# Layer 1's mixer: u tiles first, z tiles in pairs by Strassen's form, then the pool products

## The chip, the cores and the metric

The kernel runs on one core of one Trainium2 chip. The metric is the device time of one execution in microseconds (us).

## The reference

Two layers over 1024 latent tokens of width 1024, in float32. Layer 0 is a bidirectional mLSTM, which the change leaves as it is. Layer 1 is a pooling mixer, cut here to its core (the tokens are a grid of 16 rows by 64 columns; windows are 2, 4, 8 and 16, each for a group of 512 of the 2048 inner channels):

```python
u, z = split(h @ w_in, 2)                       # 1024 -> 2 x 2048
for g, w in enumerate((2, 4, 8, 16)):
    d[g] = box_mean(box_mean(u[g], w, columns), w, rows) - u[g]
y[g] = (d[g] @ w_pool[g]) * pool_scale          # 512 -> 512 in each group
out = (y * silu(z)) @ w_out
```

Around it stand a norm before (its result is h), a norm behind, and a gated residual.

## The kernel before

All data are channels on 128 partitions by tokens. Each product is made of float32 values split in a high and a low part, so one product of a 128 x 128 weight block is three matmuls (`mm3`, its matmuls have line L136) of 512 tokens. `load_w` (L138) loads a weight tile through SP's queue into `wr`, makes the high part on ScalarE (L142, `wh`) and the low part on VectorE (L144, `wl`); there are two buffers of each.

Layer 1 takes h (the tiles `h2`, 16 buffers of the tag S4: two token halves, four pairs of channel blocks, high and low) and makes 16 u tiles and 16 z tiles of 128 channels, each 2 halves x 8 blocks x 3 matmuls, then 16 pool tiles of 2 x 4 x 3. A u tile is copied by ScalarE twice from PSUM: into `U` (L1084, padded for the window) and `ur` (L1085). `box` (L1092) makes the box sums with shifted additions on VectorE: along the columns (L1097), along the rows (L1101), the scaling by the window's count (L1105, or L1109 to L1111 for window 16) and the difference from u (L1106, L1112); then the high part `a` (ScalarE, L1114) and the low part `b` (VectorE, L1115). A z tile is Silu from PSUM into `sz` (L1090). A pool tile multiplies, scales by `sz` on VectorE (L1166) and, but for the last group, stores y by POOL's queue (L1168).

The groups come one after the other: group 0's u and z tiles by halves (the second half's norm, `norm0`, is spread over the first half's matmuls by `tick`; `drain` ends it), the groups 1 to 3 whole, in the order

```python
ORDER_B = ("u0", "u1", "b0", "u2", "b1", "u3", "z0", "b2", "z1", "b3", "p0", "z2", "p1", "z3", "p2", "p3")
```

PE's order is written out by hand (`manual_schedule`) to the end of group 0's z tiles (`ctx1.close()`); elsewhere, and on the other engines and queues throughout, a planner orders the instructions. Buffers are taken by tag: `S4` has 32 of 4 KB a partition, `T5` 5, `pt` 6, `wr`, `wh` and `wl` 2 each; PSUM has `pa` 3, `pb` 2 and `pc` 3.

Layer 0 already computes its z and o tiles in pairs by a Strassen form with 7 half-size products for 8 (`strassen`, L573): weight sums on POOL, splits of each product's weights (L593), sums of products on VectorE (L601). The sums of the token blocks that it multiplies (T1, T2, T3, T4, split high and low) are made by `block_sums` (L519), stored, and loaded again by `load_sums` (L566).

Of the kernel before, what the change touches and what calls it, by code (L numbers as in the profile page):

```python
# [51 lines left out]
def hybrid_block(ctx: ExitStack, tc: tile.TileContext, xT, ctxT, vecs, w_ada0, w_ada, w_blk, w_krow, blk_mask, w_gate, w_in, b_gate, w_out,  # L52
# [490 lines left out]
    with ctx0:  # L543
# [29 lines left out]
        def strassen(src, done):  # L573


            r1, r2 = tl("wr", [P, 8, P]), tl("T5", [P, 8, P])
            nc.sync.dma_start(r1, src[0])
            nc.sync.dma_start(r2, src[1])
            a11, a12, a21, a22 = r1[:, :4], r1[:, 4:], r2[:, :4], r2[:, 4:]
            s12, s34 = tl("T5", [P, 2, 4, P]), tl("T5", [P, 2, 4, P])  # L580
            s1, s2, s3, s4 = s12[:, 0], s12[:, 1], s34[:, 0], s34[:, 1]
            G.tensor_tensor(s1, a21, a22, op=ALU.add)
            G.tensor_tensor(s2, s1, a11, op=ALU.subtract)
            G.tensor_tensor(s3, a11, a21, op=ALU.subtract)
            G.tensor_tensor(s4, a12, s2, op=ALU.subtract)
            wt = []

            def product(tag, a, b):
                i = len(wt) % 2
                wt.append((tl("wh", [P, 2, 4, P], F32R), tl("wl", [P, 2, 4, P], F32R)) if i == 0 else wt[-1])  # L590
                hi, lo = (t[:, i] for t in wt[-1])
                S.activation(hi, a, AF.Copy)  # L592
                V.tensor_tensor(lo, a, f(hi), op=ALU.subtract)  # L593
                p = pt_(tag)
                for k in range(4):
                    mm3(p, hi[:, k], lo[:, k], *b[k], k == 0, k == 3)
                return p

            def plus(p, t, d=None):
                d = tl("pt", [P, 512]) if d is None else d  # L600
                V.tensor_tensor(d, p, t, op=ALU.add)  # L601
                return d

            p = product("pa", a11, b11)
            p1 = tl("pt", [P, 512])
            S.activation(p1, p, AF.Copy)
            done(0, 0, plus(product("pc", a12, b21), p1))
            u2 = plus(product("pa", s2, tpart(2)), p1, p1)
            u3 = plus(product("pc", s3, tpart(3)), u2)
            p = product("pa", s1, tpart(1))  # L610
            done(1, 1, plus(p, u3))
            plus(p, u2, u2)
            done(1, 0, plus(product("pc", a22, tpart(4)), u3, u3))
            done(0, 1, plus(product("pa", s4, b22), u2, u2))

# [453 lines left out]
    def u_start(g):  # L1069
# [8 lines left out]
        return U, tl("S4", [P, T]), R_, C_, r0, hw  # L1078

    def u_half(ut, w, hf):  # L1080
        U, ur, R_, C_, r0, hw = ut
        p = pt_("pa")
        h2mm(p, w, hf)
        S.activation(U[:, r0 + 8 * hf:r0 + 8 * hf + 8, hw:], p.rearrange("p (r c) -> p r c", c=64), AF.Copy)  # L1084
        S.activation(ur[:, hf * 512:(hf + 1) * 512], p, AF.Copy)  # L1085

    def z_half(sz, w, hf):
        p = pt_("pc")
        h2mm(p, w, hf)
        S.activation(sz[:, hf * 512:(hf + 1) * 512], p, AF.Silu)  # L1090

    def box(ut, g, imv):  # L1092
        U, ur, R_, C_, r0, hw = ut
        win = WINDOWS[g]
# [24 lines left out]
    for g in range(4):  # L1119
        imap = tl("T5", [P, T])  # L1120
        nc.sync.dma_start(imap, inv_cnt[g:g + 1].to_broadcast([P, T]))
        imv = imap.rearrange("p (r c) -> p r c", c=64)
        ut, szs, d = [None] * 4, [None] * 4, []
        if g == 0:
            for hf in range(2):
                for j in range(4):
                    if hf == 0:
                        ut[j] = u_start(g)
                    u_half(ut[j], load_w(bw_in[4 * g + j]), hf)
                    if hf:  # L1130
                        d.append(box(ut[j], g, imv))
                for j in range(4):
                    if hf == 0:
                        szs[j] = tl("S4", [P, T])
                    z_half(szs[j], load_w(bw_in[KE + 4 * g + j]), hf)
                if hf == 0:
                    drain()
            ctx1.close()

        def u_tile(j):  # L1140
            w = load_w(bw_in[4 * g + j])
            ut[j] = u_start(g)
            for hf in range(2):
                u_half(ut[j], w, hf)

        def z_tile(j):
            w = load_w(bw_in[KE + 4 * g + j])
            szs[j] = tl("S4", [P, T])
            for hf in range(2):
                z_half(szs[j], w, hf)  # L1150

        def pool_tile(j):
# [141 lines left out]
```

## Time and profile before

| | us |
|---|---|
| median of 3 runs | 2021.52 |
| lowest and highest | 2017.68, 2022.14 |
| the profiled execution | 2018.94 |
| its span, first to last instruction | 2017.2 |
| PE (TensorE) busy in it | 1970.4 |

The profile is of one execution. PE is TensorE's matmuls, PEld its weight loads, DVE VectorE, ACT ScalarE, POOL GpSimd, SP SyncE, which only issues transfers; PEq, SPq and POOLq are the queues. The clock is the share of full speed that TensorE was granted.

### The profile page before, as it was taken

The page shows a single profiled execution, that of the slowest core. Times are in us where ns is not written, and L with a number is a line of the kernel's source. Part 1 is how long each engine was busy: PE and PEld are TensorE (multiplying, and loading weights), DVE is VectorE, ACT ScalarE, POOL GpSimd, SP SyncE. Part 2 cuts the span into 40 slices and gives each one's busy share as a digit, 9 for nine tenths or more (in the row PEclk, how much of TensorE's full clock was granted, in tenths as well). Part 3 has the DMA queues.
Part 4 walks back from the last instruction along what each step waited for, and adds up shares of the span by engine and source line. Part 5 has one row for each costly group of instructions (what it writes and reads, how often), then busy time and mean ns, then how long its engine had stood idle before and what let it go on. Part 6 is the DMA issues. An engine that isn't in the chain of part 4 may idle for free.

```text
span 2017.2 us, 26878 instructions
## 1 busy us (share of the span) xinstructions
PE 1970.4 (98%) x10050; PEld 1662.4 (82%) x10050; DVE 1287.7 (64%) x2140; ACT 807.1 (40%) x1353; POOL 419.6 (21%) x620
## 2 busy tenths in 40 slices
PE   6999999999999999999999999999999999999997
PEld 4788888788888788888888878888888888888897
DVE  4777777777767677676676662746745382943454
ACT  5477777333333433323332322534422231223443
POOL 2144434354443111111111110200000000000154
PEclk9999999999999999999999999999999999999999
DMA  9377777844444847446372414525331213142573
GB/s 365 126 256 268 266 266 269 305 157 147 131 141 142 317 136 238 154 139 232 110 261 100 152 59 156 214 92 174 95 115 56 89 42 105 43 160 100 188 241 125
DMA packets 118292, 339.49 MB, mean 168 GB/s; under 512 B 13036, under 2 KB 21740, under 8 KB 118160
## 3 DMA queue, kind: packets, MB, share of 16 engines
q1 hardware_dynamic: 90144, 242.14, 35.2%
q0 software_dynamic: 28016, 95.62, 12.8%
q8 instruction: 79, 1.29, 0.3%
q14 instruction: 53, 0.43, 0.1%
HBM read 234.77 MB, written 102.94 MB: 167 GB/s over the span
## 4 chain that ended last, share of the span: by engine, by line
PE 90%; DMA 3%; DVE 3%; ACT 2%; issue 1%; POOL 1%; SPq 0%; POOLq 0%; DVEq 0%; ACTq 0%
PE pa L136 46%; PE pc L136 35%; PE pb L136 7%; PE pb L803 2%; DVE S L923 1%; PE pc L834 1%; DMA S<-in_w_ada_dram 1%; DVE wl L144 1%; DMA S<-in_ctxT_dram 1%; DMA S<-a_d 0%; POOL S L1011 0%; DMA wr<-in_w_ada_dram 0%; DMA T<-in_bw_out_dram 0%; DMA cst<-in_w_blk_dram 0%; ACT wh L142 0%
## 5 line engine op out<-in xcount | busy, mean ns | idle before, releaser
L136 PE MATMUL pa<-S,wh 128*128 128x512 f32 (+1 forms) x2448 | 705.2, 372 | 0.0
L136 PEld LDWEIGHTS pa<-S,wh 128*128 128x128 f32 x2448 | 434.7, 189 | 67.9
L136 PE MATMUL pc<-S,wh 128*128 128x512 f32 (+1 forms) x1664 | 465.6, 366 | 3.0 <-ACT wh L142 2.2
L136 PE MATMUL pa<-S,wl 128*128 128x512 f32 (+1 forms) x1224 | 450.4, 368 | 0.0
L136 PEld LDWEIGHTS pc<-S,wh 128*128 128x128 f32 x1664 | 302.2, 190 | 54.4 <-ACT wh L142 2.4
L136 PE MATMUL pc<-S,wl 128*128 128x512 f32 (+1 forms) x832 | 303.1, 366 | 0.8 <-DVE wl L144 0.7
L144 DVE TENSOR_TENSOR wl<-wr,wh 128x1024 fp32r<-128x1024 f32 (+1 forms) x124 | 144.1, 1162 | 249.3 <-ACT wh L142 248.0
L142 ACT ACTIVATE wh<-wr 128x1024 fp32r<-128x1024 f32 (+1 forms) x124 | 124.7, 1005 | 356.8 <-PE pa L136 136.3
L136 PEld LDWEIGHTS pa<-S,wl 128*128 128x128 f32 x1224 | 230.9, 189 | 40.1 <-DVE wl L144 0.5
L136 PE MATMUL pa<-S,S 128*128 128x512 f32 (+1 forms) x1152 | 249.7, 363 | 4.3 <-DVE T L762 4.3
L136 PE MATMUL pc<-S,pt 128*128 128x512 f32 x960 | 227.6, 391 | 1.5 <-DVE S L743 1.0
L136 PEld LDWEIGHTS pa<-S,S 128*128 128x128 f32 x1152 | 192.0, 190 | 33.4 <-DVE T L762 4.5
L136 PEld LDWEIGHTS pc<-S,pt 128*128 128x128 f32 x960 | 178.0, 188 | 38.4 <-DVE S L743 1.7
L136 PEld LDWEIGHTS pc<-S,wl 128*128 128x128 f32 x832 | 157.9, 190 | 26.8 <-DVE wl L144 2.1
L805 ACT ACTIVATE pt<-pb 128x512 fp32r<-128x512 f32 (+1 forms) x96 | 47.8, 524 | 214.9 <-PE pb L803 212.6
L762 DVE SCALAR_TENSOR_TENSOR T<-pa,T 128x256 f32<-128x256 f32 (+3 forms) x184 | 78.3, 453 | 33.4 <-PE pa L136 27.2
L957 POOL TENSOR_TENSOR r4b<-r,mhalf 128x4 f32<-128x4 f32 (+1 forms) x7 | 9.2, 1320 | 389.4 <-DVE r L955 389.4
L425 ACT ACTIVATE T<-pb 128x288 f32<-128x288 f32 x160 | 63.0, 416 | 42.3 <-PE pb L136 31.9
L136 PE MATMUL pb<-S,wh 128*128 128x512 f32 x256 | 78.8, 389 | 0.0
L592 ACT ACTIVATE wh<-T 128x512 fp32r<-128x512 f32 x70 | 41.2, 626 | 93.5 <-PE pc L136 76.4
L816 DVE BATCH_NORM_STATS2 st<-pc 128x6 f32<-128x512 f32 x32 | 22.3, 698 | 83.7 <-PE pc L136 83.7
L144 DVE TENSOR_TENSOR wl<-T,wh 128x1024 fp32r<-128x1024 f32 x32 | 45.5, 1423 | 37.6 <-ACT wh L142 37.6
(341 smaller groups left out, 2606.9 us busy)
## 6 DMA issues: line engine op xcount, KB each, us to landing
wr<-in_bw_in_dram SPq DMA_DIRECT2D x40, 512.0 KB, 3.6
wr<-in_w_in_dram SPq DMA_DIRECT2D x34, 512.0 KB, 4.2
wr<-in_w_ada_dram SPq DMA_DIRECT2D x32, 512.0 KB, 4.0
wr<-in_w_out_dram SPq DMA_DIRECT2D x32, 512.0 KB, 3.6
T<-in_bw_out_dram SPq DMA_DIRECT2D x32, 512.0 KB, 4.5
S<-y_d SPq DMA_DIRECT2D x28, 512.0 KB, 7.4
vh_d<-T POOLq DMA_DIRECT2D x32, 320.0 KB, 4.7
vl_d<-T POOLq DMA_DIRECT2D x32, 320.0 KB, 4.3
```

What stands on the lines that cost most here:

```text
L136: PE.matmul(out, lhsT, rhs, start=start, stop=stop)
L142: S.activation(h, r, AF.Copy)
L144: V.tensor_tensor(l, r, f(h), op=ALU.subtract)
L425: S.activation(vst[:, :, s - s0], p, AF.Copy)
L592: S.activation(hi, a, AF.Copy)
L762: V.scalar_tensor_tensor(W[:, lo + sh:hi + sh], p[:, lo - o:hi - o], 1.0, W[:, lo + sh:hi + sh], op0=ALU.mult, op1=ALU.mult, accum_out=dp[ ...
L803: PE.transpose(p[:, j], st["M"][:, s * P:(s + 1) * P], ident)
L805: S.activation(th[:, :n], p[:, :n], AF.Copy)
L816: V.bn_stats(b6, pv)
L834: PE.transpose(p[:, c], hn[:, c * P:(c + 1) * P], ident)
L923: V.tensor_tensor(b, yraw[kp, hf], f(a), op=ALU.subtract)
L957: G.tensor_tensor(r2[:, :nb], r[:, :nb], mhalf[:, :nb], op=ALU.pow)
```

## The change

Layer 1 is ordered anew in three parts. First come all 16 u tiles, groups 3 and 2 by halves (weights loaded twice), then groups 1 and 0; each half is copied into `pt` and stored to `u_d`. The boxes of groups 3 and 2 are made beside them from u loaded back, and their high and low parts are stored (`dh_d`, `dl_d`). Beside them too, `block_sums1` makes the sums of h's blocks from `o_d`, which `next_input` now stores, and stores them in `t1_d`. Second come the z tiles, in 8 pairs by `strassen`, now an outer function; the parts 2 and 3 of T1 are loaded among the last u tiles, 1 and 4 in the first pair; Silu of z is stored in `sz_d`. Third come the pool products of groups 3, 2, 1, 0, with d and `sz` loaded back; the boxes of group 1 are made beside group 3's products and those of group 0 beside group 2's. PE's order is by hand through all of it. y of group 0 stays in SBUF, the others go through `y2_d`.

The diff, without the new DRAM tiles, the unchanged body of `strassen` that is moved, and the removed forms of the old loop:

```diff
+    def strassen(src, done, blocks, tpart, tag2):
...
+        b11, b21, b22 = blocks
+        r1, r2 = tl("wr", [P, 8, P]), tl(tag2, [P, 8, P])
...
         for n in range(0, KE, 2):
-            prod = strassen if n else plain
+            def prod(src, done):
+                if n:
+                    strassen(src, done, (b11, b21, b22), tpart, "T5")
+                else:
+                    plain(src, done)
...
+                if j:
+                    nc.gpsimd.dma_start(o_d[k - 1:k + 1, :, 512 * hf:512 * hf + 512].rearrange("j p t -> p j t"), x1[kp])
...
+    def u_half(n, w, hf):
+        p = pt_("pc" if n % 2 else "pa")
+        h2mm(p, w, hf)
+        t = tl("pt", [P, 512])
+        S.activation(t, p, AF.Copy)
+        nc.gpsimd.dma_start(u_d[n, :, hf * 512:hf * 512 + 512], t)
+
+    imvs = {}
+
+    def box(n):
+        g = n // 4
+        if g not in imvs:
+            imap = tl("T5", [P, T])
+            nc.sync.dma_start(imap, inv_cnt[g:g + 1].to_broadcast([P, T]))
+            imvs[g] = imap.rearrange("p (r c) -> p r c", c=64)
+        imv = imvs[g]
         win = WINDOWS[g]
         hw = win // 2
         R_, C_ = (16 if win == 16 else 16 + hw), 64 + hw
         r0 = R_ - 16
-        U = tl("T5", [P, R_, C_])
+        U, ur = tl("T5", [P, R_, C_]), tl("S4", [P, T])
+        nc.sync.dma_start(ur, u_d[n])
...
+        S.activation(U[:, r0:, hw:], ur.rearrange("p (r c) -> p r c", c=64), AF.Copy)
...
-        a, b = tl("S4", [P, T], F32R), tl("S4", [P, T], F32R)
+        a = tl("S4", [P, T], F32R)
         S.activation(a, ur, AF.Copy)
-        V.tensor_tensor(b, ur, f(a), op=ALU.subtract)
-        return a, b
+        nc.gpsimd.dma_start(dh_d[n], f(a))
+        V.tensor_tensor(ur.bitcast(F32R), ur, f(a), op=ALU.subtract)
+        nc.gpsimd.dma_start(dl_d[n], ur)
+
+    def block_sums1():
+        dsh1 = const([P, 4], "dsh1")
+        V.tensor_tensor(dsh1, sh1[:, 4:8], sh1[:, 0:4], op=ALU.subtract)
+        for k in range(4):
+            t0, t1 = tl("S4", [P, T]), tl("S4", [P, T])
+            for t, kk in ((t0, k), (t1, k + 4)):
+                nc.sync.dma_start(t, o_d[kk])
+            b11, b12, b21, b22 = t0[:, :512], t0[:, 512:], t1[:, :512], t1[:, 512:]
+            V.scalar_tensor_tensor(b22, b22, dsh1[:, k:k + 1], b12, op0=ALU.add, op1=ALU.subtract)
+            V.tensor_tensor(b12, b12, b11, op=ALU.subtract)
+            V.scalar_tensor_tensor(b11, b22, sh1[:, k:k + 1], b11, op0=ALU.add, op1=ALU.add)
+            V.scalar_tensor_tensor(b21, b21, sh1[:, k + 4:k + 5], b11, op0=ALU.add, op1=ALU.subtract)
+            yield
+            for j, x in ((2, b11), (3, b22), (1, b12), (4, b21)):
+                t = tl("S4", [P, 2, 512], F32R)
+                S.activation(t[:, 0], x, AF.Copy)
+                V.tensor_tensor(t[:, 1], x, f(t[:, 0]), op=ALU.subtract)
+                nc.gpsimd.dma_start(t1_d[j - 1, k], f(t))
+                if j in (3, 4):
+                    yield
+
+
+    order = [4 * g + j for g in (3, 2, 1, 0) for j in range(4)]
+    boxes = iter(order)
+    for hf in range(2):
+        for i, n in enumerate(order[:8]):
+            u_half(n, load_w(bw_in[n]), hf)
+            if hf:
+                next(sums1, None)
+                if i % 2:
+                    box(next(boxes))
+        if hf == 0:
+            drain()
+            sums1 = block_sums1()
+    T1_ = {}
+
+    def load_sums1(j):
+        for k in range(4):
+            T1_[j, k] = tl("S4", [P, 2, 512], F32R)
+            nc.sync.dma_start(f(T1_[j, k]), t1_d[j - 1, k])
+
+    for i, n in enumerate(order[8:]):
+        w = load_w(bw_in[n])
+        for hf in range(2):
+            u_half(n, w, hf)
+        next(sums1, None)
+        if i % 2 == 0:
+            box(next(boxes))
+        if i in (5, 6):
+            load_sums1(i - 3)
+
+
+    h2b = [[(h2[hf, k // 2][0][:, k % 2], h2[hf, k // 2][1][:, k % 2]) for k in range(ko, ko + 4)]
+           for ko, hf in ((0, 0), (4, 0), (4, 1))]
+
+    def sz_done(n, i, hf, t):
+        S.activation(t, t, AF.Silu)
+        nc.gpsimd.dma_start(sz_d[n + i, :, hf * 512:hf * 512 + 512], t)
+
+    def tpart1(j):
+        if (j, 0) not in T1_:
+            load_sums1(j)
+        return [(T1_[j, k][:, 0], T1_[j, k][:, 1]) for k in range(4)]
+
+    for n in range(0, KE, 2):
+        strassen([bw_in[KE + n + i] for i in range(2)], lambda i, hf, t: sz_done(n, i, hf, t), h2b, tpart1, "T5")
 
...
+    for g in (3, 2, 1, 0):
+        d = []
+        w = load_w(bw_pool[4 * g], 4)
+        for k in range(4):
+            pair = [tl("S4", [P, T], F32R) for _ in range(2)]
+            for t, src_ in zip(pair, (dh_d, dl_d)):
+                nc.sync.dma_start(f(t), src_[4 * g + k])
+            d.append(pair)
+        for j in range(4):
             n = 4 * g + j
+            if j:
+                w = load_w(bw_pool[n], 4)
             for hf in range(2):
                 s_ = slice(hf * 512, hf * 512 + 512)
+                sz = tl("pt", [P, 512])
+                nc.sync.dma_start(sz, sz_d[n, :, s_])
+                p = pt_("pc" if j % 2 else "pa")
                 for k in range(4):
                     mm3(p, w[0][:, k], w[1][:, k], d[k][0][:, s_], d[k][1][:, s_], k == 0, k == 3)
+                if g:
+                    o = sz
                 else:
                     if n % 2 == 0:
                         yraw[n // 2, hf] = tl("S4", [P, 2, 512])
                     o = yraw[n // 2, hf][:, n % 2]
+                V.scalar_tensor_tensor(o, p, vc("pool_scale", n), sz, op0=ALU.mult, op1=ALU.mult)
+                if g:
+                    nc.gpsimd.dma_start(y2_d[n - 4, :, s_], o)
+            if g > 1:
+                for _ in range(2 if j % 2 == 0 else 0):
+                    box(next(boxes))
+    ctx1.close()
...
-        for kp in range(6):
+        for kp in range(2, 8):
             yraw[kp, hf] = tl("S4", [P, 2, 512])
-            nc.sync.dma_start(yraw[kp, hf], y2_d[2 * kp:2 * kp + 2, :, s_].rearrange("j p t -> p j t"))
+            nc.sync.dma_start(yraw[kp, hf], y2_d[2 * kp - 4:2 * kp - 2, :, s_].rearrange("j p t -> p j t"))
```

## Rows read from the trace of the kernel before

**Rows 1.** The page's first part, and the span and clock of the core.
```profile
PE 1970.4 (98%) x10050; PEld 1662.4 (82%) x10050; DVE 1287.7 (64%) x2140; ACT 807.1 (40%) x1353; POOL 419.6 (21%) x620
...
core 0: 2017.2 us, clock 0.992
```

**Rows 2.** Windows: us, busy (count) of PE, PEld, DVE, ACT, POOL; clock, DMA share, GB/s.
```profile
510.19:529.24 19.05, 19.05 (x86) 15.78 (x85) 12.57 (x18) 6.90 (x13) 8.22 (x7) 1.00 0.46 152
1421.74:1813.26 391.52, 391.52 (x1729) 324.27 (x1728) 225.31 (x217) 105.78 (x152) 16.63 (x44) 1.00 0.26 86
655.00:660.00 5.00, 5.00 (x24) 4.14 (x23) 1.54 (x4) 0.63 (x1) 0.34 (x1) 1.00 1.05 404
680.00:685.00 5.00, 5.00 (x17) 3.92 (x16) 1.49 (x10) 5.00 (x11) 0.82 (x4) 0.67 1.02 417
1953.00:1958.00 5.00, 4.48 (x19) 4.19 (x20) 2.79 (x3) 1.69 (x3) 0.00 (x0) 0.51 0.92 362
1816.00:1818.00 2.00, 1.63 (x7) 1.05 (x6) 2.00 (x3) 2.00 (x4) 0.00 (x0) 1.00 0.71 227
```

**Rows 3.** The chain of waits, from 1595 us: start, us, what.
```profile
1595.82 43.52 PE pa L136 x192
```

**Rows 4.** VectorE's groups by line and shape: count, busy us, mean ns, idle before.
```profile
L593 DVE TENSOR_TENSOR wl<-T,wh 128x512 fp32r<-128x512 f32 x69 | 47.3, 708 | 0.0
L601 DVE TENSOR_TENSOR pt<-pc,pt 128x512 f32<-128x512 f32 x41 | 28.3, 691 | 43.4 <-PE pc L136 43.2
...
L1115 DVE TENSOR_TENSOR S<-S,S 128x1024 fp32r<-128x1024 f32 x16 | 19.5, 1221 | 10.6 <-ACT S L1114 10.6
```

**Rows 5.** POOL's issues of y's stores: ns min/median/max, first and last start.
```profile
L1168 POOL DMA_DIRECT2D y_d<-pt x24: 540/540/597, 1469.5 to 1705.7; - x24
```

**Rows 6.** Transfers issued between 1373 and 1814: count, KB, median us to landing.
```profile
wr<-in_bw_in_dram SPq DMA_DIRECT2D x37, 512.0 KB, 3.6
y_d<-pt POOLq DMA_DIRECT2D x24, 256.0 KB, 2.5
```

**Rows 7.** VectorE's timeline in boxes of windows 16, 8 and 4.
```profile
1717.55 5.28 DVE L1097 TENSOR_TENSOR T<-T 128x1136 f32<-128x1136 f32 x4
1722.86 4.00 DVE L1101 TENSOR_TENSOR T<-T 128x960 f32<-128x960 f32 x4
...
1728.43 0.69 DVE L1109 TENSOR_TENSOR T<-T,T 128x512 f32<-128x512 f32 x1
...
1732.72 1.22 DVE L1112 TENSOR_TENSOR S<-T,S 128x1024 f32<-128x1024 f32 x1
...
1608.75 3.82 DVE L1097 TENSOR_TENSOR T<-T 128x1072 f32<-128x1072 f32 x3
1612.60 4.08 DVE L1101 TENSOR_TENSOR T<-T 128x1216 f32<-128x1216 f32 x3
...
1499.95 2.49 DVE L1097 TENSOR_TENSOR T<-T 128x1040 f32<-128x1040 f32 x2
1502.47 2.55 DVE L1101 TENSOR_TENSOR T<-T 128x1088 f32<-128x1088 f32 x2
```

**Rows 8.** ScalarE's timeline in group 3, idle before and its releaser in brackets.
```profile
1731.92 0.60 ACT L1084 ACTIVATE T<-pa 128x512 f32<-128x512 f32 x1 [3.69 <-PE pa L136]
1734.04 1.06 ACT L1114 ACTIVATE S<-S 128x1024 fp32r<-128x1024 f32 x1 [1.52 <-DVE S L1112]
1735.00 0.58 ACT L1085 ACTIVATE S<-pa 128x512 f32<-128x512 f32 x1
...
1756.48 1.07 ACT L1114 ACTIVATE S<-S 128x1024 fp32r<-128x1024 f32 x1 [6.94 <-DVE S L1112]
1757.45 1.07 ACT L1085 ACTIVATE S<-pa 128x512 f32<-128x512 f32 x2
```

**Rows 9.** SP's timeline in layer 0, the loads of T1's parts.
```profile
345.28 19.16 SPq L566 DMA_DIRECT2D S<-t_d  x14
```

**Rows 10.** The page's second part: GB/s in 40 equal slices of the span.
```profile
GB/s 365 126 256 268 266 266 269 305 157 147 131 141 142 317 136 238 154 139 232 110 261 100 152 59 156 214 92 174 95 115 56 89 42 105 43 160 100 188 241 125
```

More of the change, by code (lines that the diff above doesn't have):

```diff
@@ L132, in hybrid_block @@
     x1_d = dr.tile([P, KD, T], F32, name="x1_d")
+    o_d = dr.tile([KD, P, T], F32, name="o_d")
+    t1_d = dr.tile([4, 4, P, 2, 512], F32, name="t1_d")
+    u_d = dr.tile([KE, P, T], F32, name="u_d")
+    dh_d = dr.tile([KE, P, T], F32, name="dh_d")
+    dl_d = dr.tile([KE, P, T], F32, name="dl_d")
+    sz_d = dr.tile([KE, P, T], F32, name="sz_d")
     y2_d = dr.tile([12, P, T], F32, name="y2_d")
@@ L440, in token_part, with product, plus @@
                 mm(gacc[ci][:32, :w], gx, ch, False, n == KE - 1)
+    def strassen(src, done, blocks, tpart, tag2):
+        b11, b21, b22 = blocks
+        r1, r2 = tl("wr", [P, 8, P]), tl(tag2, [P, 8, P])
+        nc.sync.dma_start(r1, src[0])
+        nc.sync.dma_start(r2, src[1])
+        a11, a12, a21, a22 = r1[:, :4], r1[:, 4:], r2[:, :4], r2[:, 4:]
+        s12, s34 = tl("T5", [P, 2, 4, P]), tl("T5", [P, 2, 4, P])
+        s1, s2, s3, s4 = s12[:, 0], s12[:, 1], s34[:, 0], s34[:, 1]
+        G.tensor_tensor(s1, a21, a22, op=ALU.add)
+        G.tensor_tensor(s2, s1, a11, op=ALU.subtract)
+        G.tensor_tensor(s3, a11, a21, op=ALU.subtract)
+        G.tensor_tensor(s4, a12, s2, op=ALU.subtract)
+        wt = []
+        def product(tag, a, b):
+            i = len(wt) % 2
+            wt.append((tl("wh", [P, 2, 4, P], F32R), tl("wl", [P, 2, 4, P], F32R)) if i == 0 else wt[-1])
+            hi, lo = (t[:, i] for t in wt[-1])
+            S.activation(hi, a, AF.Copy)
+            V.tensor_tensor(lo, a, f(hi), op=ALU.subtract)
+            p = pt_(tag)
+            for k in range(4):
+                mm3(p, hi[:, k], lo[:, k], *b[k], k == 0, k == 3)
+            return p
+        def plus(p, t, d=None):
+            d = tl("pt", [P, 512]) if d is None else d
+            V.tensor_tensor(d, p, t, op=ALU.add)
+            return d
+        p = product("pa", a11, b11)
+        p1 = tl("pt", [P, 512])
+        S.activation(p1, p, AF.Copy)
+        done(0, 0, plus(product("pc", a12, b21), p1))
+        u2 = plus(product("pa", s2, tpart(2)), p1, p1)
+        u3 = plus(product("pc", s3, tpart(3)), u2)
+        p = product("pa", s1, tpart(1))
+        done(1, 1, plus(p, u3))
+        plus(p, u2, u2)
+        done(1, 0, plus(product("pc", a22, tpart(4)), u3, u3))
+        done(0, 1, plus(product("pa", s4, b22), u2, u2))
     emt = const([P, 8, 36], "emt")
@@ L571, in hybrid_block @@
         b11, b21, b22 = ([h[k + ko, hf] for k in range(4)] for ko, hf in ((0, 0), (4, 0), (4, 1)))
[L573 to L614, printed above, removed]
         def z_done(n, sz, i, hf, t):
@@ L1077, in u_start @@
         G.memset(U[:, r0:, 0:hw], 0.0)
[L1078 to L1094, printed above, removed]
+        S.activation(U[:, r0:, hw:], ur.rearrange("p (r c) -> p r c", c=64), AF.Copy)
         st = 1
@@ L1112, in box @@
             V.tensor_tensor(urv, M_, urv, op=ALU.subtract)
-        a, b = tl("S4", [P, T], F32R), tl("S4", [P, T], F32R)
+        a = tl("S4", [P, T], F32R)
         S.activation(a, ur, AF.Copy)
-        V.tensor_tensor(b, ur, f(a), op=ALU.subtract)
-        return a, b
-    yraw = {}
[L1119 to L1152, printed above, removed]
@@ new lines, in tpart1 @@
+    def tpart1(j):
[4 more added lines that the diff above has]
+        strassen([bw_in[KE + n + i] for i in range(2)], lambda i, hf, t: sz_done(n, i, hf, t), h2b, tpart1, "T5")
+    yraw = {}
+    for g in (3, 2, 1, 0):
+        d = []
+        w = load_w(bw_pool[4 * g], 4)
+        for k in range(4):
+            pair = [tl("S4", [P, T], F32R) for _ in range(2)]
[3 more added lines that the diff above has]
+        for j in range(4):
```

16 lines of the change are left out of this document (removed).

## The prediction

> **What bounds the kernel now.** First the page's busy times [rows 1]: TensorE (PE) is busy 1970.4 of 2017.2 us, 98%, at a mean granted clock of 0.992; VectorE has 64%, ScalarE 40%. So the span is what TensorE is given, plus its pauses. Then the windows [rows 2]: from the start of layer 1's second token half at 1421.74 to 1813.26, where the last pool product ends, PE is busy for all 391.52 us, with 225 us of VectorE and only 86 GB/s of DMA. The stage to be changed has no pause to win, only matmuls to drop. Then the chain of waits [rows 3]: 192 matmuls of 512 columns take 43.52 us, 226.7 ns each, in the new stage too if nothing waits. The other rows tell what the new work around them costs.
>
> All sums stand against the profiled execution: 2017.2 us of span and 1.7 around it, 2018.9. The three runs go from 2017.68 to 2022.14, median 2021.52, so it is 0.1% under the median. About 0.2%, 4 us, is what can be told from no change here.
>
> **Part 1, the matmuls.** A pair of z tiles takes 2 x 48 = 96 matmuls now; Strassen's form takes 7 products of 12, 84. Eight pairs save 96 x 0.2267 = 21.8 us. Layer 0 shows what such a pair takes: 84 matmuls in 19.05 us without a pause, with VectorE busy 12.57 of it and POOL 8.22 [rows 2]. In the new z stage VectorE has 7 splits of 0.71 and 7 sums of 0.69 for each pair [rows 4], 9.8 us of 19.05; pairs 2 to 8 should run at 19.05. The pause behind the last pool product, 0.37 of the 2.00 us from 1816 [rows 2], may go with y of one group staying in SBUF: 0.4. **-22.2 us.**
>
> **Part 2, box sums behind the u tiles and the first z pair.** Eight wide groups' boxes now run beside 130.6 us of u tiles (t = 0 at the second half pass; 8 x 5.44 + 8 x 10.88). A box no longer takes u from PSUM: ScalarE copies it out (0.59), POOL issues a store (0.54) that lands 2.5 us later [rows 5, 6], SP loads it back (3.6, as a weight load of the same size), ScalarE copies it into U (1.06). Box 12 starts at 5.44 + 0.59 + 0.54 + 2.5 + 3.6 + 1.06 = 13.7.
>
> To its high part `a`, a box of window 16 costs VectorE 5.28 + 4.00 + 3 x 0.69 + 1.22 = 12.6, one of window 8 3.82 + 4.08 + 2 x 1.22 = 10.3 [rows 7]: 91.6 us for eight. Other VectorE work in the stage: 14 weight splits and 8 low parts of a box, both of 1024 columns and 1.22, 27, and block sums, 32 operations of 512 columns and 0.69 [rows 4], 22: 49.
>
> Between boxes there is a gap that before did not have. The trace shows buffers of one tag being given out in program order: with half of S4's 32 buffers free, ScalarE's second copy of u (L1085) starts at 1735.00 though its twin from the same PSUM tile (L1084) ran at 1731.92; in between stands the previous box's `a` at 1734.04, whose buffer is asked for earlier in the program. At 1757.45 two such copies again stand right behind an `a` [rows 8]. By that order a box's reload is placed behind the `a` of the box before: 3.6 + 1.06 + 0.3, 5 us, seven times, 35. So the last wide box ends between 13.7 + 91.6 + 35 = 140 (all other work fits in the gaps) and 13.7 + 91.6 + 35 + 49 = 189 (none does). I take the middle, 164, 34 us after the u tiles' end.
>
> What is late next is the first z pair. T1 parts 3, 1 and 4 stand behind box 11's `a` in the same tag, and SP has the second pair's weights (whose T5 buffer is the window map that box 11 reads last) ahead of them. They are 12 loads of 512 KB: 14 such took 19.16 us in layer 0 [rows 9], 1.37 each; at the 266 GB/s of the mixed slices in the page's fourth to seventh slice [rows 10] 1.97. I take 1.7: 20.4, and 2 to land. Product 6 needs the last of them, then come 3.4 us of matmuls: the pair ends 34 + 20.4 + 2 + 3.4 = 60 after the u tiles instead of 19. **+41 us**; with 140 and 1.37 it is 9.4 + 16.4 + 5.4 - 19 = 12, with 189 and 1.97 it is 58.4 + 23.6 + 5.4 - 19 = 68.
>
> **Part 3, the pool products, 87.0 us of PE.** Their inputs now come from DRAM: d 24 x 0.524 MB for three groups (the first group's can come in the z stage), eight reloads of u 4.2, dh and dl stores 8.4, sz 8.4, y2 6.3, pool weights 4.2, yraw 3.1: 47 MB. At some 400 GB/s, the best 5 us windows (404 and 417 [rows 2]), this takes 118 us, 31 more than PE; at 417 and without yraw 18. Before, this whole stage moved 86 GB/s.
> The order of buffers makes a chain of it as well. Box 4's reload can start when the last z pair's second product has freed h2's buffers, 13.6 us before the stage, so the box starts at -8.6. Four boxes of window 4 (2.49 + 2.55 + 2 x 1.22 = 7.5 each [rows 7]), three low parts and eight evictions of 0.7 to 0.75 put the last `a` at -8.6 + 30 + 3.7 + 5.5 = 31. The next group's d stands behind it in the tag: 8 loads at 1.37 less a first product's 2.7 and 2 to land, 10. Group 2 starts at 41 and not 21.8: 19. Boxes 0 to 3 stand behind these loads: 11 + 5 to the first, 4 x 4.9 (four operations of 1.22) + 3.7 + 4 to the last `a`, 10 for d: 53 after 31, against 41 + 21.8: 21. So 40 with no gap between boxes, 70 with gaps of 5. I take **+39**, near the low end, since it is also nearest to the bytes' 31; bounds 18 and 70.
> The Trainium skill ("HBM Reference", Specifications (TRN2)) gives about 358 GB/s as a core's effective share of HBM; by it, as an estimate, the 47 MB take 131 us and the stall is 44. This trace's windows at 404 and 417 GB/s lie above that figure, as the same page of the Trainium skill says of a core that streams alone, so the rows decide.
>
> **Part 4, the clock after a pause.** Where PE starts again after a pause the granted clock is low: 17 matmuls between 680 and 685 at 0.67, where 226.7 ns would make 22, and 0.51 between 1953 and 1958 [rows 2]. That is 1 to 3 us for each long pause; with some three of them **+4** (1 to 6).
>
> **At nothing.** POOL's extra work: 72 issues of 0.54 beside the u tiles (u 32, o 8, T1 16, dh and dl 16), 39 of 130 us, and 8.2 of 19.05 us in a pair; behind a late store only the box that reloads it waits, already counted. ScalarE's extra copies, 1.06 for a box and 0.6 for half a u tile, lie beside 391 us of which it is busy for 106 [rows 2]; without that cover each would add itself to a box. The moved norm0 of half 1 keeps its place beside the first half pass, with 4 more POOL issues.
>
> **Sum.** 2018.9 - 22.2 + 41 + 39 + 4 = 2080.7, **2080**.
>
> **Rivals.**
> (a) *Boxes end in time, the pool stage alone stalls.* If other work fits in the gaps and SP's queue lets reloads go ahead of the `a` (the order is shown on ScalarE's own queue, not across to SP), box 11 ends by some 140 and the first pair loses 12 or less. 2018.9 - 22.2 + 6 + 29 + 2 = 2034, about 2015 to 2050. For it: SP's loads do not wait for ScalarE. Against: the seven reloads still need their u copies on ScalarE behind the `a`.
> (b) *Faster: reloads and d run ahead.* One mechanism, buffers given as they come free and not in program order. Then T1 loads during the u tiles (it needs only the 16 free S4 buffers and 2 x 4 of h2's), boxes 4 to 7 and their d go into the z stage, where VectorE has 74 us and the DMA nearly all its time to spare, and nothing is late. 2018.9 - 22.2 and up to 13 of leftovers, 1997 to 2010. It is decided at pair 1: if product 4 starts within 8.2 us of the pair's start, behind no T1 load issued after box 11's `a`. Against it speak the copies at 1735.00 and 1757.45 [rows 8].
> (c) *The savings are just eaten*, 2015 to 2023: a between-case of (a) and (b), with no mechanism of its own.
> That fewer matmuls are not issued is no rival: the count falls from 10050 by 96 in any case.
>
> **Chances.** Forecast (both stages stall) 0.70, 2080, by the bounds 2018.9 - 22.2 + 12 + 18 + 1 = 2028 to 2018.9 - 22.2 + 68 + 70 + 6 = 2141, likely 2045 to 2125; (a) 0.14; (b) 0.12; (c) 0.04. Faster is (b), 0.12, same (c), 0.04, slower the rest, 0.84. The range leaves out (b) and the upper edge: 2012 to 2128.
>
> **What the profile after would show.** Right: z pairs 2 to 8 at 19.05 us; a pause of 20 us or more in the first pair, ended by DMA into S4 with T1 loads issued behind box 11's `a`; pauses ahead of groups 2 and 1 of the pool products, the DMA busy for nearly all of that stage at 350 GB/s or more; a granted clock near 0.5 to 0.7 behind each. Wrong if there is no pause in the first pair (the order of buffers then does not bind SP), if a z pair takes more than 19.05 throughout (POOL's or VectorE's new work binds), or if the u tiles themselves wait (for `pt` buffers that a slow store holds).

## The result and the profile after

The changed kernel takes 2133.86 us (median of 4, 2132.22 to 2139.18) against 2019.6 of the kernel before beside it: a ratio of 1.0575, interval 1.0559 to 1.0591. Forecast were 2080 and a range to 2128: the side was right, the size too small, and the time lies above the range. The profiled execution took 2132.22 us, with a span of 2130.2, 113.0 more than before [rows 1]. All times below are from the profiled execution of each kernel, which lay 7 to 8 us above the median of its runs in e3 and e4, 6 below in e15 and within 3 elsewhere.

The page's first part and the core's clock:

```profile
PE 1970.5 (93%) x9954; PEld 1648.8 (77%) x9954; DVE 1369.4 (64%) x2269; ACT 838.2 (39%) x1401; POOL 531.4 (25%) x772
...
core 0: 2130.2 us, clock 0.963
```

The 96 matmuls are gone (9954 of 10050), and yet PE is busy as long as before: the 21.8 us that they took went to other matmuls, at a mean clock of 0.963 instead of 0.992. Windows, with the columns of [rows 2]: the u tiles from the second half pass on, the first z pair, the second pair, pairs 2 to 8, the pool products, then two stretches of these:

```profile
1422.90:1555.05 132.15, 130.86 (x578) 108.03 (x577) 103.43 (x108) 47.11 (x65) 28.14 (x59) 1.00 0.72 263
1555.05:1629.04 73.99, 28.88 (x86) 18.51 (x85) 48.69 (x42) 15.49 (x22) 23.04 (x22) 0.65 0.68 252
1629.04:1648.09 19.05, 19.05 (x86) 15.78 (x85) 8.96 (x14) 6.90 (x13) 7.63 (x8) 1.00 0.33 115
1629.04:1762.32 133.28, 133.28 (x590) 110.36 (x589) 63.52 (x98) 48.06 (x83) 46.02 (x57) 1.00 0.38 128
1762.32:1925.66 163.34, 99.74 (x386) 75.41 (x385) 91.29 (x98) 29.88 (x36) 23.48 (x50) 0.77 0.85 304
...
1782.00:1814.00 32.00, 10.82 (x28) 5.65 (x26) 24.38 (x24) 6.44 (x7) 4.83 (x16) 0.63 0.98 359
...
1841.00:1865.00 24.00, 0.00 (x0) 0.00 (x0) 11.03 (x9) 3.71 (x4) 1.30 (x3) 0.50 0.65 224
```

The u tiles take 132.2, 1.6 more than the forecast's 130.6, with one wait of 1.3; seven z pairs take 19.04 each, without a pause, as layer 0's pair did [rows 2]. The first pair takes 73.99, 54.9 more than a pair; the pool products take from 1762.32 to 1925.66, 163.3 us, 76.3 more than their 87.04. With the 21.8 us saved, a start of the second half pass 1.2 us later and a tail 0.6 us longer than before this is the whole difference: -21.8 + 1.6 + 54.9 + 76.3 + 1.2 + 0.6 = 112.8, the 113.0 but for rounding. The 1.2 is no effect that I can put down to the change: between profiles of kernels with the same work ahead of that place, the first u eviction lies anywhere from 1376.7 to 1385.2.

What PE waited for (us in total, times, longest), in the first pair and then in the pool products:

```profile
PE pc L142 <- DMA S<-t_d: 31.6, 8, 27.6
PE pa L142 <- ACT wh L469: 11.6, 1, 11.6
...
PE pa L142 <- DMA S<-dh_d: 55.5, 4, 35.7
PE pa L142 <- DMA S<-dl_d: 6.3, 8, 1.7
PE pa L142 <- DVE wl L150: 1.6, 1, 1.6
```

In the first pair it is T1 (`t_d`), by one wait of 27.6 us ahead of product 4, and 11.6 for the weight sum of product 3. POOL makes this sum in a T5 tile and starts it at 1567.92, just as box 9's last operation on U ends; that it waited for U's T5 buffer is argued from these times. The 11.6 us cost nothing of their own, since product 4 could not start ahead of T1 anyway. In the pool stage it is d: one wait ahead of group 2 (17.2) and one ahead of group 1 (35.7). With two short ones in the first pair these waits sum to 45.0 of 54.9 and 63.4 of 76.3; what is left of both, 23 us, goes with matmuls at the low clock.

SP's queue over the first pair, then ScalarE's copy that ends the last wide box:

```profile
1544.68 16.34 SPq L1173 DMA_DIRECT2D S<-t_d  x4
1561.18 0.32 SPq L1105 DMA_DIRECT2D S<-u_d  x1
1585.94 0.33 SPq L455 DMA_DIRECT2D T<-in_bw_in_dram  x1
1588.15 0.33 SPq L454 DMA_DIRECT2D wr<-in_bw_in_dram  x1
1601.61 0.33 SPq L455 DMA_DIRECT2D T<-in_bw_in_dram  x1
1602.03 12.43 SPq L1173 DMA_DIRECT2D S<-t_d  x12
...
1601.58 1.06 ACT L1129 ACTIVATE S<-S 128x1024 fp32r<-128x1024 f32 x1 [14.05 <-DVE S L1121]
```

Here is the forecast's step as it was put: the 12 loads of T1 stand behind a later pair's weights (L455), and these go at 1601.61, when box 11 gives back its T5 buffer; PE has been waiting for T1 since 1578.8.

### The profile page after: what moved, and what is told of

It reads as the page before. It is cut to its first block, busy times and chain, and to the rows that moved or that the text cites. A ratio compares the mean times of both kernels' runs of the same rounds, so it can differ in the third digit from the quotient of the medians.

```text
span 2130.2 us, 27514 instructions
## 1 busy us (share of the span) xinstructions
PE 1970.5 (93%) x9954; PEld 1648.8 (77%) x9954; DVE 1369.4 (64%) x2269; ACT 838.2 (39%) x1401; POOL 531.4 (25%) x772
## 4 chain that ended last, share of the span: by engine, by line
PE 77%; DMA 8%; DVE 7%; issue 4%; ACT 2%; POOL 1%; SPq 1%; POOLq 0%; DVEq 0%; ACTq 0%
PE pa L142 41%; PE pc L142 31%; PE pb L142 3%; DMA S<-u_d 2%; PE pb L816 1%; DMA S<-t_d 1%; DVE T L1112 1%; DVE T L1116 1%; DMA wr<-in_w_ada_dram 1%; DMA T<-in_bw_out_dram 1%; DMA S<-dl_d 1%; PE pc L847 1%; DVE wl L150 1%; DVE S L1121 1%; DMA S<-xl_d 1%
## 5 line engine op out<-in xcount | busy, mean ns | idle before, releaser
L142 PE MATMUL pa<-S,wh 128*128 128x512 f32 (+1 forms) x2576 | 756.8, 377 | 74.4 <-DMA S<-dh_d 55.5
L142 PEld LDWEIGHTS pa<-S,wh 128*128 128x128 f32 x2576 | 462.3, 191 | 158.7 <-issue 53.7
L142 PE MATMUL pc<-S,wh 128*128 128x512 f32 (+1 forms) x1728 | 487.8, 368 | 35.4 <-DMA S<-t_d 31.6
L142 PE MATMUL pa<-S,wl 128*128 128x512 f32 (+1 forms) x1288 | 479.9, 373 | 4.0 <-DVE wl L150 2.9
L150 DVE TENSOR_TENSOR wl<-wr,wh 128x1024 fp32r<-128x1024 f32 (+1 forms) x108 | 124.5, 1153 | 150.3 <-ACT wh L148 149.8
L148 ACT ACTIVATE wh<-wr 128x1024 fp32r<-128x1024 f32 (+1 forms) x108 | 107.5, 996 | 281.7 <-PE pc L142 123.7
L469 ACT ACTIVATE wh<-T 128x512 fp32r<-128x512 f32 x110 | 64.7, 626 | 156.9 <-PE pc L142 127.6
L478 DVE TENSOR_TENSOR pt<-pc,pt 128x512 f32<-128x512 f32 x66 | 45.6, 691 | 106.7 <-PE pc L142 81.4
L478 DVE TENSOR_TENSOR pt<-pa,pt 128x512 f32<-128x512 f32 x88 | 58.5, 686 | 43.9 <-PE pa L142 43.8
L1112 DVE TENSOR_TENSOR T<-T 128x1024 f32<-128x1024 f32 (+6 forms) x40 | 52.4, 1309 | 36.4 <-ACT T L1109 35.8
```

Of the source, the lines that this page charges most:

```text
L142: PE.matmul(out, lhsT, rhs, start=start, stop=stop)
L148: S.activation(h, r, AF.Copy)
L150: V.tensor_tensor(l, r, f(h), op=ALU.subtract)
L1112: V.tensor_tensor(U[:, r0:, 0:C_ - st], U[:, r0:, 0:C_ - st], U[:, r0:, st:C_], op=ALU.add)
```

## The experiments

Two stretches serve below, told by three marks: the last eviction of a u tile (ScalarE), the last Silu of z and the last scaling of a pool product (VectorE): after the change these start at 1555.1, 1766.1 and 1926.0, so 211.0 us for z and 159.9 for the pool products; with no pause they would be 156 and 84. Where the expectations speak of 52 us for the first pair, the windows above have 54.9.

**e1, `a` in a tag of its own; e2, U in a tag of its own.**

```diff
-        a = tl("S4", [P, T], F32R)
+        a = tl("AB", [P, T], F32R)          # e1: one buffer
-        U, ur = tl("T5", [P, R_, C_]), tl("S4", [P, T])
+        U, ur = tl("UB", [P, R_, C_]), tl("S4", [P, T])   # e2: two buffers
```

> The high part a of a box gets a tag of its own with one buffer, instead of one of S4's 32; nothing else changes. Theory of the prediction (buffers of a tag are given in program order, so the reload of the next box, the T1 loads and the d loads all stand behind a): reloads and T1 loads are issued ahead of a, the pause in the first z pair falls from 52 us to under 20 and those in the pool stage from 76 to some 45, total 2133.9 - 35 - 30 = 2069, between 2045 and 2090. Rival (they stand in SP's queue behind loads into T5, which wait for a box's U): U is as before, so both pauses stay within 8 us, 2126 to 2142.

> The padded tile U of a box gets a tag of its own with two buffers, instead of one of T5's five; a stays in S4. Theory of the queue behind T5: loads into T5 no longer wait for a box's end, so the reload behind them starts earlier and the T1 loads too; the first pair's pause falls from 52 to some 30, the pool stage's from 76 to some 50: 2133.9 - 48 = 2086, between 2070 and 2100. Theory of the program order in S4: reload, T1 and d still stand behind a; within 8 us of 2133.9.

Measured: e1 2066.56 (ratio 1.0231, 1.0216 to 1.0246), e2 2139.25 (1.0595, 1.0571 to 1.062). Both are as the theory of the program order has them. The place of `a` in S4's order is worth 67 of the 114 us. (e1 also has one buffer more. But S4 was not full: from 1573 on, when the last of the sums was stored and SP still waited, its 32 buffers held at most h2's 16, four of T1's 16 and six of three boxes.) SP's timeline of e1 has 12 of the 16 T1 loads beside the u tiles, from 1484 to 1542, and the last four at the first pair's start; some of its lines:

```profile
1484.14 4.44 SPq L1173 DMA_DIRECT2D S<-t_d  x3
...
1500.72 4.12 SPq L1173 DMA_DIRECT2D S<-t_d  x5
...
1557.57 2.31 SPq L1173 DMA_DIRECT2D S<-t_d  x4
```

z takes 172.1 and the pool products 126.5. In e2, SP's waits from 1555 to 1607 show how the order acts:

```profile
SPq L455 <- DVE UB L1120: 38.0, 1, 38.0
SPq L1173 <- DMA t_d<-S: 7.1, 1, 7.1
```

Again a load of weights into T5 is ahead of T1's in the queue; with U out of T5 it waits for the window's map, which box 11 reads last (L1120). So the semaphore that SP waits at is one of T5; that T1 is queued behind it comes of S4's order, and of the two edits only e1's takes it away. The rival is right on the wait, wrong on what would cure it. Had T1 waited on S4 itself, SP's wait would stand at L1173. In the pool stage e2's two pauses are 32.1 and 24.0 us instead of 17.2 and 35.7: U's place moves them without making their sum less.

**e3, two boxes deferred; e4, z tiles whole.**

```diff
-        if i % 2 == 0:
+        if i in (0, 2):
             box(next(boxes))
...
     for n in range(0, KE, 2):
         strassen(...)
+        if n in (2, 6):
+            box(next(boxes))
```

> The boxes of tiles 10 and 11 are moved behind the second and the fourth z pair; the rest as after the change. Theory that T1's loads wait for the end of the last box ahead of them: the last such box is now that of tile 9, whose a came 13 us after the u tiles' end and not 47, so the first pair's pause falls from 52 us by some 35 to about 15, and the z pairs with a box lose less than 5: total 2133.9 - 35 + 3 = 2102, between 2090 and 2112. Rival (the 16 T1 loads and the stores beside them are too many bytes for that stretch): the pause stays over 35, total over 2115.

> The z tiles are made whole, without Strassen's form (96 more matmuls of 226.7 ns, 21.8 us), and T1's sums and loads are left out; the order u, z, pool products and all spills of u, d and sz stay. Theory that the first pair's 52 us are T1's wait: 2133.9 - 52 + 21.8 = 2103, some 2 less for the clock, 2095 to 2108, with the pool stage as it was (76). Rival (boxes, or T5 buffers that they hold, stop the first z tiles anyway): over 2115. If the pool stage's pauses came of T1, they would fall too: under 2090.

Measured: e3 2103.02 (1.0418, 1.0396 to 1.0441), inside the theory's range: z takes 180.6, of which the first pair loses 25 us, 16.5 of them in waits for T1; the pool products take 164.6, no less than before. That is the wait for the last box ahead of T1, singled out. e4 2043.29 (1.0123, 1.01 to 1.0146), 60 less than the 2103 expected: z takes 175.8, its 174.1 without a pause; but the pool products fall to 115.5 too. T1 fills 16 of S4's 32 buffers beside h2's, so that the boxes of group 1, behind d in S4's order, cannot start before the last z pair; without T1 they run beside the z tiles (copies into U at 1599.0 to 1637.5, and 1757.1 to 1804.0 after the change). Part of the pool stage's pauses came of T1's room: the last of the cases set out, to which the prediction gave no price. e4 leaves out T1's transfers and the form's work on VectorE too; that it is the room alone is argued from the order.

**e5, e6, e7: the boxes' places.** e5 moves six boxes into the z stage; e6 is e5 with `a` and U in tags of one buffer each; e7 is e6 with group 3's `sz` kept in S4.

```diff
     for n in range(0, KE, 2):
         strassen(...)
+        if n in (2, 4, 6, 8, 10, 12):      # tiles 10, 11, 4, 5, 6, 7
+            box(next(boxes))
...
-            if g > 1:
-                for _ in range(2 if j % 2 == 0 else 0):
-                    box(next(boxes))
+            if g == 3:
+                box(next(boxes))
```

> The change's tags as they are, only the places of boxes differ: tiles 8 and 9 beside the last u tiles, 10, 11, 4, 5, 6, 7 behind the second to seventh z pair, 0 to 3 one behind each product of group 3. Theory (a chain in S4's program order, with both pauses on it): the first pair's pause is as with two boxes deferred, some 22 us; in the pool stage only boxes 0 to 3 stand ahead of group 2's d, last a some 45 us after the stage's start, d 10 later, so one pause of 33 instead of two of 76 in all: 2133.9 - 30 - 43 = 2061, 2045 to 2080. Rival (bytes alone set the pool stage): moving boxes takes at most 6 MB of it away, 15 us: over 2085.

> The same places of boxes, and a and U each with a tag of one buffer. Theory: no reload, T1 load or d load stands behind a box's end; the first pair's pause falls to some 10, and the pool stage is left with its bytes, d 12.6, sz 8.4, u 2.1, dh and dl 4.2, y 6.3, weights 4.2, yraw 3.1, 41 MB, 102 us at 400 GB/s against 87: 15. 2133.9 - 42 - 61 - 3 = 2028, 2012 to 2042. Rival (VectorE's order, boxes ahead of the splits and sums that PE waits for): pairs with a box take 2 to 4 us longer, six of them, over 2040.

> As e6, and the gates of the last two z pairs (tiles 12 to 15, group 3) stay in four S4 buffers instead of being stored and loaded: 2.1 MB less in the pool stage, 2.1 less ahead of it. Theory of the bytes: 5 us less than e6, 3 to 9. Rival (S4 is full, so the kept gates hold up boxes or d): not less than e6, or more.

Measured: e5 2089.38 (1.0352, 1.0329 to 1.0375), over the theory's 2080 and in the rival's range, yet not by the rival's reason: the pool stage has the one pause forecast, 28.6 ahead of group 2, and 134.6 in all, while z takes 190.1, with pairs that wait for a split behind a box (4.7 us at most). e6 2051.03 (1.0162, 1.0142 to 1.0182), over the theory's 2042, is the best with Strassen's form, still 32 us behind the kernel before and by the medians 8 behind e4, which has 96 matmuls more (the intervals of these two just overlap): z takes 176.8, with 12.3 us of waits for weight splits (the rival's way), and the pool products 106.8, with one wait of 19.2 for weights. PE no longer waits for T1. e7 2052.66 (1.0172, 1.0154 to 1.0191), the rival's case: not less than e6, with z 8 us shorter, the pool products 12 longer, and 6.7 us of waits for d that e6 has not. 2 MB less brought nothing in sum.

**e8, e9, e10: fewer bytes, with the chain gone.** e8 is e1 without the loads of dl in groups 2 to 0; e9 is e1, e10 is e6 with all of y kept in S4.

```diff
-            pair = [tl("S4", [P, T], F32R) for _ in range(2)]
+            pair = [tl("S4", [P, T], F32R) for _ in range(2 if g == 3 else 1)]   # e8
...
-                if g:
-                    o = sz
+                o = yraw[n // 2, hf][:, n % 2]                                   # e9, e10
```

> As e1 (a with a tag of its own), and the low parts dl of groups 2, 1 and 0 are not loaded back: the high part stands in for them in the products, so part of the computation is left out; 6.3 MB less in the pool stage. Theory that its remaining 43 us of pauses in e1 are bytes: 6.3 / 0.4 = 16 us less than e1's 2066.6, 2048 to 2056. Rival (VectorE's boxes ahead of the weight splits): within 5 of e1, over 2061.

> As e1 (a with a tag of its own), and y of all groups stays in S4 buffers instead of going out and back: 6.3 MB of stores and the loads of yraw, 3.1 MB of them by the first half of the output product, are gone. Theory that bytes hold e1's pool stage (at 370 to 412 GB/s from 1756 to 1840): some 15 to 20 us less than 2066.6, 2045 to 2053. Rival (weight splits late behind the boxes on VectorE, 20 us of e1's pauses): bytes matter for at most the rest, under 8 us, over 2058.

> As e6 (boxes in the z stage, a and U with their own tags), and y of all groups stays in S4. Theory of the bytes: e6's pool stage, at 409 GB/s ahead of its one pause of 19 us, has some 32 MB left of 41, 80 us at 400 against 87 of PE: the pause goes but for 5; 2051 - 18 = 2033, 2026 to 2040. Rival (the weight tile is late because SP issues 16 loads of d ahead of it, whatever else moves): the pause stays over 12, over 2043.

Measured: e8 2055.69 (1.0186, 1.0166 to 1.0206), 11 less than e1 and just inside the theory's range, though only 6 of them in the pool stage (120.4); nearly all the rest came ahead of the z tiles. What bytes do there once the chain is gone is seen better in e1 itself: from 1756 to 1840 its DMA is full (395 GB/s, share 1.02), while PE is busy for 62.7 of these 84 us. e9 2068.74 (1.0247, 1.0231 to 1.0263), 2 more than e1; e10 2060.69 (1.0205, 1.0188 to 1.0222), 10 more than e6: the pool products take 139.2 and 123.1. Both lie in their rivals' ranges. Keeping y costs S4 what it saves in bytes: d waits for its buffers, and PE for d in pieces (29 us in 18 waits for dh and dl in e9). As tests of bytes e9 and e10 say little.

**e11, e12** (e10 with the low part on POOL; the same with the wide boxes beside the u tiles again).

```diff
-        V.tensor_tensor(ur.bitcast(F32R), ur, f(a), op=ALU.subtract)
+        G.tensor_tensor(ur.bitcast(F32R), ur, f(a), op=ALU.subtract)
```

> As e10, and the low part of a box is made by POOL instead of VectorE: 1.22 us less on VectorE for each of 16 boxes. Theory that z pairs with a box lose 2 us each because PE waits for a weight split behind a box's operations: half of it back, 4 to 8 us less than e10. Rival (POOL, which makes the weight sums, becomes late instead): not less than e10.

> As e11, but the boxes of tiles 10 and 11 are beside the last u tiles again and only 4 to 7 stand in the z stage, behind the third to the sixth pair. Theory: four narrow boxes of 8.7 us fit a pair's free 9 on VectorE where a wide one of 11.5 does not, which saves 4 of the wide boxes' some 5 us, but the last wide box costs the first pair some 10 as in e1: e11 + 6, within 2 to 10. Rival (wide boxes are the main loss of the z stage): e11 - 5 or less.

Measured: e11 2071.1 (1.0262, 1.0246 to 1.0279), 10 more than e10, the rival's way; e12 2069.17 (1.0246, 1.0231 to 1.0261), e11 - 2: neither case. PE's waits for weight splits grow in e11 from 10.4 to 14.7 us; why is not shown.

**e13, e14: chain and bytes apart, on the changed kernel.**

```diff
-        while st < win:
+        while st < win and g > 1:                                        # e13
...
                 nc.sync.dma_start(sz, sz_d[n, :, s_])
+                nc.sync.dma_start(tl("hn", [P, 512]), sz_d[n, :, s_])     # e14
```

> As after the change, but the boxes of groups 1 and 0, those of the pool stage, leave out their shifted additions (part of the computation is left out): 5 us less VectorE for each of four and 2.5 for each of the other four; the bytes are the same. Theory that the pool stage's 160 us are the chain box, reload, box, d: 4 x 5 + 4 x 2.5 = 30 less, for what of the first boxes is ahead of the stage some 5 less of that: 2133.9 - 27 = 2107, 2098 to 2115. Rival (the 47 MB set it, as the prediction's choice of 39 leaned on): its 118 us stay the floor, but the pause moves by less than 10: over 2123.

> As after the change, and each half of sz is loaded a second time in the pool stage, into a buffer that nothing reads: 32 more loads of 256 KB, 8.4 MB, 21 us of transfer at 400 GB/s; 32 x 0.33 us more issuing on SP. Theory of the chain: its links get a little slower where transfers overlap, 3 to 10 us more, 2137 to 2144. Rival (bytes): 2133.9 + 21 = 2155, over 2149.

Measured: e13 2115.76 (1.0474, 1.0455 to 1.0493), 18 less, between the two cases and just over the chain's range; e14 2154.31 (1.0666, 1.065 to 1.0682), 20 more, in the bytes' case. PE's waits for dh in e13, then in e14, and the extra loads of e14 (count, ns, first and last start):

```profile
PE pa L142 <- DMA S<-dh_d: 40.5, 4, 25.9
PE pa L142 <- DMA S<-dh_d: 76.3, 4, 38.4
L1218 SPq DMA_DIRECT2D hn<-sz_d x32: 319/320/673, 1735.3 to 1826.9; - x32
```

The two pauses answer differently. Ahead of group 2, 17.2 us became 12.3 in e13 and 38.4 in e14; ahead of group 1, 35.7 became 25.9 in e13 and 36.5 in e14. The boxes of group 1 were lighter by 20 us in all, and the first pause fell by 5; those of group 0 by 10, and the second fell by 10. Windows of e13 over its first stretch of the pool stage, and of e14 over its two pauses:

```profile
1764.00:1796.00 32.00, 19.74 (x88) 16.03 (x87) 18.61 (x21) 8.79 (x10) 8.92 (x23) 0.85 1.01 393
```

```profile
1785.00:1823.00 38.00, 0.00 (x0) 0.00 (x0) 22.65 (x20) 5.80 (x6) 5.28 (x17) 0.53 0.96 349
1856.00:1892.00 36.00, 0.18 (x1) 0.21 (x1) 16.51 (x15) 5.80 (x6) 4.29 (x8) 0.54 0.75 253
```

Up to the first pause's end the DMA is nearly always busy (share 0.96 to 1.01), and the boxes matter little: transfers decide there. Whether it is their bytes alone, or SP's queue too, e14 does not tell apart: eleven of its extra loads stand directly ahead of group 2's d in that queue, from 1802.3 to 1815.5. In the second pause the DMA is not full (0.75 in e14, 0.65 after the change), and what the boxes lose PE gains: the chain of four boxes decides. e14 is no test of that pause, since the last of its extra loads was issued at 1826.9, ahead of it.

**e15, pool weights through ScalarE's queue, on e6.**

```diff
-        nc.sync.dma_start(r, src)
+        (nc.scalar if kk == 4 else nc.sync).dma_start(r, src)
```

> As e6, but the pool products' weights are loaded through ScalarE's queue instead of SP's, where 16 loads of d stand ahead of them. Theory that e6's one pause of 19 us in the pool stage is this order: the pause falls below 8, 2051 - 12 = 2039, 2033 to 2045. Rival (those transfers are one pool of bandwidth, and the weights land as late from any queue; or ScalarE's own copies stand ahead of the issue): over 2046.

Measured 2057.97 (1.0184, 1.0168 to 1.02), not faster than e6; the pause is 22.1 instead of 19.2. This is the rival's range, but it does not tell the cases apart: ScalarE stood still for 17 us ahead of the two loads, issued them at 1746.6 and 1748.0, and split the first only at 1761.7, behind two copies into U that waited for VectorE. What e6's last pause is due to stays open.

## Why the prediction was wrong

**Right.** The matmuls: -21.8 in the z stage; the hoped 0.4 behind the last pool product is not to be seen in a tail that is 0.6 longer. Both places of the stalls, what PE waits for in each, and the buffer order behind the first: e1 gives back 67 us, e3 31 by the boxes alone, e2 nothing. The bytes of the pool stage: 49.7 MB for 47. Rival (b), which needed buffers out of program order, and (a) fall with product 4, which starts 51 us after the pair's start and not 8.2. Pairs 2 to 8 are free of pauses, the u tiles but for 1.3 us. One sign did not come: the DMA was to be busy for nearly all of the pool stage at 350 GB/s or more, and has a share of 0.85 and 304.

**The first pair: 41 forecast, 54.9 measured (45.0 of it waits), inside 12 to 68.** Box 11's `a` came 179 us after the second half pass began, not 164. From each `a` to the next box's copy into U it took 39.4 us for seven gaps and 7.4 for the copies, 47 for my 35, of which two gaps make 24: one reload stood behind a weight load in SP's queue, and one copy into U behind the last u tile's eviction on ScalarE:

```profile
1542.30 1.06 ACT L1129 ACTIVATE S<-S 128x1024 fp32r<-128x1024 f32 x1 [2.93 <-DVE S L1121]
...
1555.14 0.60 ACT L1088 ACTIVATE pt<-pc 128x512 f32<-128x512 f32 x1 [1.95 <-issue]
1555.63 1.05 ACT L1109 ACTIVATE T<-S 128x1024 f32<-128x1024 f32 x1
```

The 12 loads took 23 us from their issue, for 22.4.

**The pool stage: 39 forecast, 63.4 us of waits measured, 76.3 with the low clock behind them. This is the step that failed.** The prediction had a chain (40, or 70 with a gap of 5 between boxes) and the bytes (31), and took the chain without gaps since the bytes were near it, as if the larger of two bounds held over the whole stage. Each holds a part of it: transfers up to group 2's start, the chain of boxes 0 to 3 from there to group 1's. After the change, SP's queue ahead of group 2's d and the high parts of boxes 6 and 7; then box 2's `a`, box 3's reload, copy into U and `a`, and the first load of group 1's d:

```profile
1795.51 0.55 SPq L1105 DMA_DIRECT2D S<-u_d  x1
1796.15 0.38 SPq L1208 DMA_DIRECT2D S<-dh_d  x1
1802.98 1.06 ACT L1129 ACTIVATE S<-S 128x1024 fp32r<-128x1024 f32 x1 [7.74 <-DVE S L1121]
1812.85 1.06 ACT L1129 ACTIVATE S<-S 128x1024 fp32r<-128x1024 f32 x1 [7.86 <-DVE S L1121]
...
1852.56 1.06 ACT L1129 ACTIVATE S<-S 128x1024 fp32r<-128x1024 f32 x1 [5.14 <-DVE S L1121]
1853.13 0.37 SPq L1105 DMA_DIRECT2D S<-u_d  x1
1858.26 1.06 ACT L1109 ACTIVATE T<-S 128x1024 f32<-128x1024 f32 x1 [4.64 <-DMA S<-u_d]
1864.46 1.06 ACT L1129 ACTIVATE S<-S 128x1024 fp32r<-128x1024 f32 x1 [5.14 <-DVE S L1121]
1864.96 0.42 SPq L1208 DMA_DIRECT2D S<-dh_d  x1
```

Ahead of group 2, 19 us were forecast and 17.2 came, and the group started 41 us into the stage as forecast, but by luck: d was to stand behind box 7's `a`, put at 31. That `a` came at 51, and SP issued d 17 us ahead of it. What SP stood at before were loads of `sz`, for 9.5 of the 15 us from 1782, until y's stores gave back `pt` buffers, with the DMA at 0.98. Ahead of group 1, 21 were forecast and 35.7 came. There d does stand behind the last `a`, and the gaps that were put at nothing are real: summed with them, the prediction's own chain has 36 ahead of this group (its 70 is 34 and 36).

The chain's links are transfers among others, not the lone ones of the rows that priced them. After the change, from issue to landing (median, in the pool stage):

```profile
S<-dh_d SPq DMA_DIRECT2D x12, 512.0 KB, 10.3
S<-dl_d SPq DMA_DIRECT2D x12, 512.0 KB, 11.0
...
S<-u_d SPq DMA_DIRECT2D x7, 512.0 KB, 6.5
```

A reload of u took 6.5 us for the 3.6 of [rows 6]; box 0's, behind eight loads of d, took 12.6. Each reload of boxes 1 to 3 waits for the box before (issues at 1823.59, 1838.53 and 1853.13, each within 0.6 us of that box's `a`), 12 to 15 us a box where I had 6.1, or 11 with a gap. The Trainium skill ("HBM Reference", Specifications (TRN2)) has some 358 GB/s as a core's effective share; in the stretches where transfers decide the trace has 349 to 393 on the mean. The 44 us estimated from that page of the Trainium skill for this stage were nearer than my 39, but not by its rule: in the stretch that cost most the DMA was at 0.65.

**The clock: 4 forecast, some 23 by the difference above.** I had priced two restarts of layer 0 and the tail. Here there are four long pauses, and behind three of them PE goes on in pieces, matmul by matmul as d or T1 lands, with a granted clock of 0.51 to 0.55 over windows of 15 us.

**The range.** Of the 51 us between the forecast and the profiled time, 24 are the pool stage's waits, 19 the clock, 4 the first pair's waits and 4 the rest. The sum of the high bounds was 2141; the range stopped at 2128 and the time is 2133.9. The waits lay inside their bounds (45.0 in 12 to 68, 63.4 in 18 to 70), the clock did not (23 for 1 to 6). To stop short of the sum's upper end was the other mistake: the three late terms went the same way, since longer pauses also bring more of the low clock.

## What to carry to other kernels

A buffer that is asked for late in program order holds back what is asked for after it in the same tag, loads for other stages too, by way of the order in which a queue gets its loads; give such a buffer a tag of its own before anything else is moved. When a stage has a chain and a byte bound, lay both over its parts and add up the larger of each part; here one bound for the whole was too low. Saving matmuls of a kernel that is 98% PE-bound by spilling its inputs pays only when reloads are ready a stage ahead: in the best order found with the form 22 us of matmuls were saved for 54 us of pauses, and the change's own order without the form (e4) took some 8 us less.
